# Softmax over 32768 columns: the last two stores moved behind the last load on SyncE's queue, and a 512 B packet per DMA engine written at once

## Chip, cores, metric

One core of one Trainium2 chip. The time is the device time of one execution in microseconds. Executions of the same kernel differ, so medians are given with their number of runs and their spread. Each batch of experiments ran on one chip together with the kernel before; the batches ran on different chips.

## The reference

```python
def reference(logits, temperature):            # logits (16, 256, 32768) float32, temperature 1.0
    scaled = logits / temperature
    scaled = scaled - scaled.max(axis=-1, keepdims=True)
    exp_scaled = np.exp(scaled)
    return (exp_scaled / exp_scaled.sum(axis=-1, keepdims=True)).astype(np.float32)
```

## The kernel before

Each row of 32768 is halved, which gives 8192 rows of 16384 values: 64 tiles of 128 partitions, 64 KB (one row) per partition, 8.4 MB per tile. Three buffers hold three tiles. SyncE issues the loads, ScalarE the stores. A tile is treated in pieces: VectorE takes the maximum of a piece, ScalarE its exponential and sum; the pieces and the two halves of a row are combined by small VectorE instructions; then VectorE and ScalarE share the scaling, in place.

(Shortened: lines joined, comments added.)

```python
_LOAD = 16384
_PIECES = (4096, 4096, 4096, 2048, 2048)
_ON_DVE = (4096, 4096, 2048, 0, 0)
_END = 4096
_FINE_STORES = 3
    def load(t):
        n = _END if t in (0, G - 1) else _LOAD          # first and last tile in four pieces
        for s in range(0, W, n):
            nc.sync.dma_start(out=buf[t % _BUFS][:, s : s + n], in_=x[t * P : (t + 1) * P, s : s + n])

    def store(t, a, b):
        n = _END if t >= G - _FINE_STORES else b - a    # last three tiles in pieces of 16 KB per row
        for s in range(a, b, n):
            nc.scalar.dma_start(out=o[t * P : (t + 1) * P, s : s + n], in_=buf[t % _BUFS][:, s : s + n])
    # ... (combine, normalise: max, exp, combine, scale; normalise(1) issues store(0) after its first exp,
    #      normalise(t) ends with store(t), the last tile stores each piece as soon as it is scaled)
    with tc.manual_schedule():
        for t in range(_BUFS):
            load(t)
        for t in range(G):
            normalise(t)
            if t and t + _BUFS - 1 < G:
                load(t + _BUFS - 1)
```

## Time and profile before

| | before |
|---|---|
| time, median of 3 | 2496.59 us (2495.63 to 2496.76) |
| span of the profiled execution | 2493.4 us |
| busy: VectorE, ScalarE | 63%, 55% |
| DMA | 431 GB/s, full in every slice but the last |

The prediction shows and reads the lines. How to read them: q1 and q10 are the DMA queues of SyncE and ScalarE. In the table of windows the last two columns are the share of the 16 DMA engines that was busy and the rate in GB/s. A packet is one transfer in the records, mostly 64 KB (a whole row) or 16 KB (a piece of one). It counts with its whole duration in the window in which it begins, so single short windows may exceed 1.

### The profile page before, as it was taken

To read this page: it belongs to the slowest core of one execution; us is meant where nothing else is said; L and a number is where in the kernel's file an instruction comes from. 1 tells how busy PE (TensorE), PEld (TensorE's weight loads), DVE (VectorE), ACT (ScalarE), POOL (GpSimd) and SP (SyncE) were. 2 spreads that over 40 slices of the span, in tenths; PEclk is the share of its full clock that TensorE was granted. 3 is DMA by queue.
4 is the path that set the end of the run, shared out by engine and by line. 5 is a ranking of instruction groups with operands and counts; after the bars stand their busy time and mean duration, and the time that the engine had idled before them with its cause. 6 is when DMAs were issued, how large, how long until landed. Compare 5 with 4: busy or idle time off the path is not lost.

```text
span 2493.4 us, 2622 instructions
## 1 busy us (share of the span) xinstructions
DVE 1575.8 (63%) x1216; ACT 1367.7 (55%) x895; POOL 0.2 (0%) x4
## 2 busy tenths in 40 slices
DVE  6575665766657666575665755657656566575665
ACT  6464645646556465464554645546455464554654
POOL 0000000000000000000000000000000000000000
DMA  9999999999999999999999999999999999999998
GB/s 421 433 424 436 435 437 424 436 434 437 424 436 435 437 424 436 433 428 435 434 430 433 434 436 427 433 436 431 429 435 437 423 435 437 427 431 437 425 429 379
DMA packets 20612, 1073.91 MB, mean 431 GB/s; under 512 B 2288, under 2 KB 2288, under 8 KB 2288
## 3 DMA queue, kind: packets, MB, share of 16 engines
q10 hardware_dynamic: 10512, 536.88, 49.9%
q1 hardware_dynamic: 10080, 536.88, 49.9%
q14 instruction: 20, 0.16, 0.0%
HBM read 536.87 MB, written 536.87 MB: 431 GB/s over the span
## 4 chain that ended last, share of the span: by engine, by line
DMA 75%; DVE 15%; ACT 9%; issue 0%; SPq 0%; DVEq 0%; ACTq 0%
DMA x<-in_logits_dram 38%; DMA out_dram<-x 37%; DVE nm L103 11%; ACT x L110 7%; DVE x L142 3%; ACT x L146 2%; DVE f L138 0%; SPq L63 0%; ACT ee L123 0%; DVE rS L137 0%; DVE Sh L82 0%; DVE ttj L126 0%; DVE Sh L79 0%; DVEq L191 0%; ACTq L71 0%
## 5 line engine op out<-in xcount | busy, mean ns | idle before, releaser
L103 DVE TENSOR_REDUCE nm<-x 128x1 f32<-128x4096 f32 x318 | 1117.5, 3579 | 678.0 <-DMA x<-in_logits_dram 678.0
L110 ACT ACTIVATE x<-x,nm 128x4096 f32<-128x4096 f32 x318 | 965.3, 3036 | 1026.2 <-DVE nm L103 1013.6
L146 ACT ACTIVATE x<-x,f 128x2048 f32<-128x2048 f32 (+1 forms) x194 | 371.2, 1975 | 75.4 <-DVE f L138 74.1
L142 DVE TENSOR_SCALAR x<-x,f 128x4096 f32<-128x4096 f32 (+2 forms) x194 | 372.2, 1975 | 2.5 <-DVE f L138 0.2
L126 DVE CUSTOM_DVE_ANT_0 ttj<-ee,ssum 128x5 f32<-128x5 f32 (+1 forms) x64 | 10.6, 166 | 203.0 <-ACT ee L123 203.0
L110 ACT ACTIVATION_READ_ACCUMULATOR x<-x,nm 128x1 f32 x318 | 59.2, 186 | 0.0
L123 ACT ACTIVATE ee<-nm,nMh 128x5 f32<-128x5 f32 (+1 forms) x64 | 18.1, 283 | 0.0
L138 DVE TENSOR_SCALAR f<-ee,rS 128x5 f32<-128x5 f32 (+1 forms) x64 | 14.8, 231 | 2.2
L137 DVE RECIPROCAL rS<-Sh 128x1 f32<-128x1 f32 x64 | 10.5, 164 | 2.2
L82 DVE TENSOR_TENSOR nMh<-nMh 128x1 f32<-128x1 f32 x64 | 10.2, 160 | 2.2
L82 DVE TENSOR_TENSOR Sh<-Sh 128x1 f32<-128x1 f32 x64 | 10.2, 159 | 2.2
L121 DVE TENSOR_REDUCE nMh<-nm 128x1 f32<-128x5 f32 (+1 forms) x64 | 10.1, 157 | 2.2
L79 DVE STREAM_SHUFFLE nMh<-nMh 128x1 f32<-128x1 f32 x64 | 9.7, 151 | 0.0
L79 DVE STREAM_SHUFFLE Sh<-Sh 128x1 f32<-128x1 f32 x64 | 9.7, 151 | 0.0
L110 ACT ACT_TABLE_LOAD x1 | 1.3, 1283 | 8.1 <-DMA x<-in_logits_dram 8.1
L126 DVE DVE_READ_ACCUMULATOR2_ANT Sh<- 128x1 f32 x64 | 5.3, 83 | 0.0
L79 DVE LOAD_MASK_SELECT Sh<-Sh x64 | 0.9, 14 | 2.8
L79 DVE LOAD_MASK_SELECT nMh<-nMh x64 | 0.9, 14 | 2.8
L177 POOL MEMSET const-bfloat16-1.0<- 128x1 bf16 x1 | 0.1, 101 | 0.0
L177 POOL MEMSET const-uint8-127<- 128x1 uint8 x1 | 0.1, 101 | 0.0
L177 POOL MEMSET const-float32-0.0<- 128x1 f32 x1 | 0.1, 98 | 0.2 <-issue 0.2
L177 POOL MEMSET const-float32-1.0<- 128x1 f32 x1 | 0.1, 98 | 0.0
## 6 DMA issues: line engine op xcount, KB each, us to landing
out_dram<-x ACTq DMA_DIRECT2D x12, 2048.0 KB, 19.3
x<-in_logits_dram SPq DMA_DIRECT2D x8, 2048.0 KB, 18.4
x<-in_logits_dram SPq DMA_DIRECT2D x62, 43.6
out_dram<-x ACTq DMA_DIRECT2D x61, 44.3
```

The source lines that it names most:

```text
L79: nc.vector.stream_shuffle(out=v[:, j + 1 : j + 2], in_=v[:, j : j + 1], mask=mask)
L82: nc.vector.tensor_tensor(out=v[:, j + 1 : j + 2], in0=v[:, j : j + 1], in1=v[:, j + 1 : j + 2], op=op,)
L103: nc.vector.tensor_reduce(out=nm[:, k : k + 1], in_=xc, axis=X, op=A.max, negate=True)
L110: nc.scalar.activation(out=xc, in_=xc, func=Exp, bias=nm[:, k : k + 1], scale=inv_t, accum_out=ssum[:, k : k + 1],)
L121: nc.vector.tensor_reduce(out=nMh[:, 0:1], in_=nm, axis=X, op=A.min)
L123: nc.scalar.activation(out=ee, in_=nm, func=Exp, bias=nMh[:, n_rounds : n_rounds + 1], scale=-1.0)
L126: nc.vector.tensor_tensor_reduce(out=ttj, in0=ee, in1=ssum, scale=1.0, scalar=0.0, op0=A.mult, op1=A.add, accum_out=Sh[:, 0:1],)
L137: nc.vector.reciprocal(out=rS, in_=Sh[:, n_rounds : n_rounds + 1])
L138: nc.vector.tensor_scalar_mul(out=f, in0=ee, scalar1=rS)
L142: nc.vector.tensor_scalar_mul(out=xs[:, a:b], in0=xs[:, a:b], scalar1=f[:, k : k + 1])
L146: nc.scalar.activation(out=xs[:, b:c], in_=xs[:, b:c], func=Copy, scale=f[:, k : k + 1])
L177: nc = _bacc.Bacc("TRN2", target_bir_lowering=False, num_devices=1)
```

## The change

Its intent is to keep the DMA engines busy at the end (the last load no longer shares them with the store of tile 62, and ScalarE no longer stands in its waits), and to pay for the first use of the store queue early.

```diff
-_FINE_STORES = 3
+_TOUCH = 128
+    touch = pool.tile([16, _TOUCH], fp32, tag="touch", name="touch")
     def store(t: int, a: int, b: int) -> None:
-        n = _END if t >= G - _FINE_STORES else b - a
-        for s in range(a, b, n):
-            nc.scalar.dma_start(
-                out=o[t * P : (t + 1) * P, s : s + n],
-                in_=buf[t % _BUFS][:, s : s + n],
-            )
+        engine = nc.sync if t >= G - 2 else nc.scalar
+        engine.dma_start(
+            out=o[t * P : (t + 1) * P, a:b], in_=buf[t % _BUFS][:, a:b]
+        )
     with tc.manual_schedule():
+        nc.vector.memset(touch, 0.0)
         for t in range(_BUFS):
             load(t)
+        nc.scalar.dma_start(out=o[:16, :_TOUCH], in_=touch)
         for t in range(G):
```

Store 61 stays on ScalarE's queue but goes out as whole rows of 64 KB; store 62 is one DMA on SyncE's queue; store 63 keeps its four pieces, on SyncE's queue.

## The prediction

> **What bounds the kernel now.** I read the page's slices and queue shares first, then the chain of waits, then the time line of the last 60 us, then short windows at both ends, and last the packet records of the trace.
>
> ```profile
> DMA  9999999999999999999999999999999999999998
> DMA packets 20612, 1073.91 MB, mean 431 GB/s; under 512 B 2288, under 2 KB 2288, under 8 KB 2288
> q10 hardware_dynamic: 10512, 536.88, 49.9%
> q1 hardware_dynamic: 10080, 536.88, 49.9%
> ```
>
> The 16 DMA engines are full in every slice but the last; q1 holds the loads (issued by SyncE), q10 the stores (issued by ScalarE), and each takes half of the engines' time. So this is a DMA-bound stream, and only idle or stretched DMA time can be won. In the packet records a 64 KB packet (one partition's whole row) takes 2.418 us and a 16 KB packet 0.611 us. Each engine has to move 67.1 MB: 16 engines at 65,536 B in 2.418 us make 433.7 GB/s, and 1073.7 MB at that rate take 2476 us. The span is 2493.4 us, the measured time 2496.59 us, so some 3.2 us lie outside the span and at most 17 us inside it could be anything but plain transfer. 2% would be 50 us: not to be had.
>
> Where the 17 us are: about 9.5 us per engine are 64 KB packets that ran longer than 2.418 us (scattered, except one cluster, below); 1.75 us pass before the first packet; some 1.3 us follow the last; the rest is a hole near the end. The hole in windows (columns: busy time by engine, clock, DMA share, GB/s):
>
> ```profile
> 2462.00:2464.00 2.00, 0.00 (x0) 2.00 (x1) 0.00 (x0) 1.00 1.03 442
> 2464.00:2466.00 2.00, 0.00 (x0) 2.00 (x3) 0.00 (x0) 1.00 0.82 352
> 2466.00:2467.00 1.00, 0.00 (x0) 1.00 (x1) 0.00 (x0) 1.00 0.31 131
> 2467.00:2468.00 1.00, 0.00 (x0) 1.00 (x1) 0.00 (x0) 1.00 0.15 66
> 2469.00:2470.00 1.00, 0.69 (x5) 0.23 (x1) 0.00 (x0) 1.00 0.08 33
> 2471.00:2472.00 1.00, 1.00 (x2) 0.44 (x2) 0.00 (x0) 1.00 0.00 0
> 2472.00:2473.00 1.00, 1.00 (x2) 1.00 (x1) 0.00 (x0) 1.00 0.84 360
> ```
>
> Most engines run dry at 2465.5 to 2467 and start again at 2472.4, with the store of the last tile (63). A share of about 0.06 is one engine of sixteen: one engine goes on alone until 2470.4 (its packets end at that time in the records). Why the last store is late:
>
> ```profile
> 2439.82 13.70 ACTq L71 DMA_DIRECT2D out_dram<-x  x3
> 2440.89 17.39 DVE L103 TENSOR_REDUCE nm<-x 128x1 f32<-128x4096 f32 x4
> 2453.56 3.71 ACT L110 ACTIVATE x<-x,nm 128x4096 f32<-128x4096 f32 x1 [12.54 <-DMA x<-in_logits_dram]
> ...
> 2468.34 0.28 ACT L123 ACTIVATE ee<-nm,nMh 128x4 f32<-128x4 f32 x1
> ...
> 2471.52 0.34 ACTq L71 DMA_DIRECT2D out_dram<-x  x1
> ```
>
> ScalarE is stuck from 2439.8 to 2453.5 in issuing tile 62's store. The program order says why: its four pieces reuse the completion semaphores of the four pieces of load 63, so each piece waits until one of those has landed. All four exponentials of tile 63 then run in a row after 2453.56 (14.9 us), though VectorE had its maxima ready one by one from 2445.3.
>
> **What the Trainium skill says.** "DMA: Bandwidth & Descriptors", section "Queues, rings and completion order": each DMA engine takes turns between the queues that have work, one packet at a time. The trace agrees. In 2404 to 2408 us, with 64 KB load packets against mostly 16 KB store packets, q1 has 68.4% and q10 17.2% of the engines (packets counted by start); from 2414 to 2450, both with 16 KB, 51.2% and 49.8%. The same page, "Issuing engines are not separate DMA queues": DMAs issued from different engines run on the same 16 engines. Agrees: q10 alone from 2456 to 2464 moves 436 GB/s, no less than both together, so moving stores to SyncE's queue costs no bandwidth. Same page, "Where 436 GB/s comes from": a ceiling of 435 GB/s; the 433.7 above is that ceiling for practical purposes. I found nothing there on the first use of a queue, which the added packet is about.
>
> **The change part by part.**
> (1) Store 62 goes from ScalarE's queue to SyncE's, behind load 63, as one DMA. ScalarE no longer stands in its semaphore waits. The compiled order shows no such wait left on ScalarE; the pieces of store 63 wait for semaphores of load 62, store 60 and the first two pieces of load 63, all landed by then. Load 63 no longer shares the engines with store 62, only with store 61. Store 61 has 64 KB packets now and load 63 16 KB ones, so the load gets about a fifth until store 61 is through, then everything: both are done at the same sum. From before: everything up to store 62 was done at 2466 (2470.4 on the slow engine), and store 62 is 8 rows of 2.418 = 19.35 us per engine, so load 63 lands near 2446.5 (2451 on the slow engine) instead of 2453.1. Tile 62 is computed at 2441.0, so store 62 is in the queue in time and no hole opens there.
> (2) The end of tile 63 then hangs on VectorE: its four maxima start at 2440.89, after tile 62's scaling, and end at 2458.32 as before (the last piece would have to land after 2453.9 to delay them). Then exp 3.78, and from the ee exponential to the first store issue 3.18 as before (2468.34 to 2471.52): 2458.35 + 3.78 + 3.18 = 2465.3 instead of 2471.5, that is 6.2 us earlier; first packets at about 2466.2 (0.85 us after the issue, as before).
> (3) The fast engines now hardly idle: dry at about 2465.5, fed at 2466.2. They gain about 6.2 us. But the slow engine idled only from 2470.4 to 2472.4. It gains 2.0 us, and the end is the slowest engine's: the last packet goes from 2492.05 to 2490.05. The 0.1 to 0.2 us spread of landings at the end of before is an effect of the hole, which let the slow engine catch up.
> (4) Stores 61 and 62 as 64 KB packets: 16 rows per engine, each 4 x 0.611 - 2.418 = 0.026 us cheaper, 0.42 us; six semaphore packets of 9 ns fewer, 0.05 us. An instruction-fetch packet (8 KB, 0.31 to 0.47 us) that fell into the hole may now cost an engine 0.3 us. Net +0.2 us won.
> (5) The added packet. In before the first store is issued at 46.52, and the 16 load packets that begin at 48.4 to 48.8 take 2.9 to 3.6 us instead of 2.418, on average 0.94 us more on all 16 engines. The windows show it as the one share over 1 at the same GB/s:
>
> ```profile
> 40.00:45.00 5.00, 2.94 (x1) 0.00 (x0) 0.00 (x0) 1.00 0.97 419
> 45.00:50.00 5.00, 5.00 (x2) 3.48 (x1) 0.00 (x0) 1.00 1.16 419
> 50.00:55.00 5.00, 5.00 (x2) 4.12 (x4) 0.00 (x0) 1.00 0.97 419
> ```
>
> That looks like a price of the store queue's first use. The first load packets at 1.75 us likewise take about 1.25 instead of 0.611 us. The added store (16 rows of 512 B, one per engine, after a VectorE memset of about 0.1 us) should be issued near 0.9 us and reach the engines near 2.2 us, where they are still slow with the loads' own start. If the two first-use prices overlap, up to 0.94 us is won; if not, the price is only moved, and nothing is won. I take 0.6. The packet itself is under 0.1 us per engine; the wait of store 0 on its landing is over 40 us early.
>
> Sum: 2.0 + 0.2 + 0.6 = 2.8 us; 2496.6 - 2.8 = 2493.8 us.
>
> **Rivals.** (a) The lag of the slow engine is chance and not a property of the run: then the end moves with the first store's issue, 6.2 + 0.2 + 0.6 = 7.0 us, 2489.6 us. For it: only one trace. Against it: the eighteen 8 KB instruction-fetch packets of 0.309 us between 100 and 2342 us make 5.6 us, near the 4.5 us of lag, if one engine carries them all; which engine carried a packet is not recorded. And store landings show one engine 6.5 to 8 us after the first nearly everywhere. (b) Load 63, at a fifth of the engines, lands later than 2453.9 and delays VectorE's last maximum, so ScalarE's freedom is worth less: 2495 to 2497 us. Against it: the sum of bytes ahead of it is smaller than before. (c) The first-use price is tied to the first large write, not to the queue: the touch wins nothing, 2494.4 us. (d) SyncE's queue with loads and stores in a row stalls at the change of direction: 1 to 2 us, about 2495.5 us. (e) The steady stream changes its rhythm by the shift of semaphores and timing: it is at the ceiling, so only the scattered 9.5 us can move, by perhaps 1 us either way.
>
> **Range and chances.** The centre is 2493.8; (a) pulls down, (b) and (d) up, and runs of before spread by 1.1 us. 8 in 10: 2489.3 to 2496.4. Within 2% is practically certain: 0.5% each side is for a fault that I don't see.
>
> **What the profile of after would show.** Step 1: no ScalarE wait near 2440 to 2453, load 63 landed by about 2452. Step 2: the first store of tile 63 issued near 2465 (less what the touch wins). Step 3: no window with DMA share under 0.9 between 2440 and 2485, but the last 5 us of transfers running on one or a few engines, the landings of the last stores spread by 4 to 5 us instead of 0.2. Step 5: the window 45 to 50 us back at 0.97 and the DMA share or GB/s of the first 5 us a little worse. Wrong: if the last landings lie close together and the end is 6 to 7 us earlier, rival (a); if the stretched packets at 48 us remain, rival (c).

## The result

The changed kernel took 2496.78 us (median of 4 runs: 2502.03, 2498.99, 2494.58, 2493.97), the kernel before in the same comparison 2496.21 (4 runs, 2495.63 to 2496.76). The ratio is 1.0005, 95% interval 0.9986 to 1.0024: the same. "Within 2%" was right, but 2496.78 lies outside the predicted range of 2489.3 to 2496.4, by 0.4 us.

The profiled execution is the slowest of the four. From its page: traffic, queues, and the landings of the stores and of the added packet (last column: us from issue to landing).

```profile
span 2500.3 us, 2620 instructions
DMA packets 19781, 1073.93 MB, mean 430 GB/s; under 512 B 2208, under 2 KB 2224, under 8 KB 2224
q1 hardware_dynamic: 10800, 553.65, 51.4%
q10 hardware_dynamic: 8960, 520.11, 48.5%
...
out_dram<-touch ACTq DMA_DIRECT2D x1, 8.0 KB, 5.8
out_dram<-x SPq DMA_DIRECT2D x1, 28.6
```

16.8 MB of stores moved from q10 to q1, and the added packet landed 5.8 us after its issue. (Its packets reached the engines at 5.4 to 5.9 us, not near 2.2 us as forecast, so they missed the slow start of the loads that they were to overlap with.) The engines were as full as before, yet the span is 6.9 us longer. The issue of the last load in the kernel before, and the end of the execution of the changed one, from their time lines (start, duration, engine):

```profile
2410.02 2.31 SPq L63 DMA_DIRECT2D x<-in_logits_dram  x4
```

```profile
2418.12 2.53 SPq L65 DMA_DIRECT2D x<-in_logits_dram  x4
2450.99 28.75 SPq L73 DMA_DIRECT2D out_dram<-x  x5
...
2455.29 3.71 ACT L111 ACTIVATE x<-x,nm 128x4096 f32<-128x4096 f32 x1 [4.33 <-DVE nm L104]
...
2468.27 3.71 ACT L111 ACTIVATE x<-x,nm 128x4096 f32<-128x4096 f32 x1 [0.52 <-DVE nm L104]
2471.97 0.28 ACT L124 ACTIVATE ee<-nm,nMh 128x4 f32<-128x4 f32 x1
```

and from its windows:

```profile
45.00:50.00 5.00, 5.00 (x2) 3.43 (x1) 0.00 (x0) 1.00 1.18 419
...
2472.00:2474.00 2.00, 1.53 (x8) 0.85 (x3) 0.00 (x0) 1.00 0.00 0
2474.00:2475.00 1.00, 1.00 (x2) 1.00 (x2) 0.00 (x0) 1.00 0.15 66
2475.00:2476.00 1.00, 1.00 (x1) 1.00 (x1) 0.00 (x0) 1.00 0.58 246
...
2496.00:2497.00 1.00, 0.00 (x0) 0.00 (x0) 0.00 (x0) 1.00 0.08 33
2497.00:2498.00 1.00, 0.00 (x0) 0.00 (x0) 0.00 (x0) 1.00 0.08 33
```

Three readings. First, the end does what was forecast, only later. SyncE issues load 63 as soon as store 60 has landed: at 2418.12 here, at 2410.02 in the kernel before, so 8.1 us of delay had gathered before the changed part began. ScalarE's exponentials now follow VectorE's maxima one by one, and the first piece of store 63 was issued at 2475.01, which is 56.9 us after load 63's issue; in before it was 2471.52 - 2410.02 = 61.5 us. (A share of 0.00 in 2472 to 2474 doesn't mean idle engines: their packets had begun before. The packet records have fifteen of them dry at about 2473.6 and fed again at 2475.9: 2.2 us, where 0.7 was forecast.) Second, the last stretch of transfers is that of one engine alone (one of sixteen is a share of 0.06; the windows show 0.08, as a packet counts where it begins), as forecast. Third, the window at 45 to 50 us still shows a share of 1.18 at 419 GB/s: the stretched packets at the first store are all there.

So what is to be explained is the 8 us lost in the stream of tiles, which the change hardly touches, and the scatter of 8 us between four runs.

### The profile page after: what moved, and what is told of

The parts are those of the page before. It is cut to its first block, busy times and chain, and to the rows that moved or that the text cites. A ratio compares the mean times of both kernels' runs of the same rounds, so it can differ in the third digit from the quotient of the medians.

```text
span 2500.3 us, 2620 instructions
## 1 busy us (share of the span) xinstructions
DVE 1575.7 (63%) x1217; ACT 1367.8 (55%) x895; POOL 0.2 (0%) x4
## 4 chain that ended last, share of the span: by engine, by line
DMA 73%; DVE 16%; ACT 9%; another core or an unknown queue 2%; issue 0%; SPq 0%; ACTq 0%
DMA x<-in_logits_dram 37%; DMA out_dram<-x 36%; DVE nm L104 12%; ACT x L111 7%; DVE x L143 3%; ACT x L147 2%; DVE f L139 0%; ACT ee L124 0%; DVE rS L138 0%; DVE Sh L83 0%; DVE ttj L127 0%; DVE Sh L80 0%; SPq L65 0%; ACTq L196 0%
## 5 line engine op out<-in xcount | busy, mean ns | idle before, releaser
L127 DVE CUSTOM_DVE_ANT_0 ttj<-ee,ssum 128x5 f32<-128x5 f32 (+1 forms) x64 | 10.6, 166 | 196.8 <-ACT ee L124 196.8
```

The source lines that it names most:

```text
L127: nc.vector.tensor_tensor_reduce(out=ttj, in0=ee, in1=ssum, scale=1.0, scalar=0.0, op0=A.mult, op1=A.add, accum_out=Sh[:, 0:1],)
```

## Experiments

Two measures come from the trace's packet and semaphore records. *Stretched time*: the durations of the 64 KB packets beyond 2.418 us, summed and divided by 16 engines. *Tail*: from the landing of store 60 on the slowest of the 16 engines to the last landing of all. Up to store 60 both kernels do the same work but for the added packet, so the tail isolates the moved stores. A DMA has sixteen landings, one semaphore update from each engine. The records don't name the engine: "the slowest engine" is the last of the sixteen updates, and that it is the same engine from one DMA to the next is supposed.

### Is the scatter the kernel's own? (the change repeated, and each part alone)

The changed kernel again, no edit:

> The changed kernel as it is, five rounds beside the kernel before, to see whether its spread (2493.97 to 2502.03 us in four runs, against 2495.63 to 2496.76) is its own. Theory A (the steady stream of this kernel varies because of the added packet, which sets another rhythm of the two queues from the start): spread over 5 us again, median 2495 to 2499. Theory B (the spread was chance of that chip or that hour): spread under 2 us and a median of 2493 to 2495, as predicted. In the profile the load packets near 48 us should again be stretched by about 1 us under both.

The added packet alone:

```diff
 (kernel before; cut: _TOUCH and the tile touch, as in the change)
+        nc.vector.memset(touch, 0.0)
         for t in range(_BUFS):
             load(t)
+        nc.scalar.dma_start(out=o[:16, :_TOUCH], in_=touch)
```

> The kernel before plus the added packet alone (memset and one 16 x 512 B store at once; the stores of the end untouched). Theory A: the wide spread comes along, 2496 to 2504 us, median 2498 or more, with 12 us or more of stretched 64 KB packets per engine in the profile (9.5 in before). Theory B: like before, 2495.5 to 2497 us.

The moved stores alone:

```diff
 (changed kernel)
-        nc.vector.memset(touch, 0.0)
-        nc.scalar.dma_start(out=o[:16, :_TOUCH], in_=touch)
```

> The changed kernel without the added packet: only the stores of the last tiles changed. Up to 2400 us it is the kernel before. Theory A: narrow spread and 2493 to 2494.5 us, 2 to 3 us under before. Theory B: the same time as the changed kernel, 2493 to 2495 us. A third theory (C: the moved stores win nothing, as the slow engine decides): 2495.5 to 2497 us.

Measured in one batch, all correct: before 2496.92 (11 runs, 2493.32 to 2503.99); changed 2493.96 (5 runs, 2492.19 to 2497.0), ratio 0.9986 [0.9971, 1.0001]; packet alone 2493.41 (5 runs, 2492.52 to 2497.4), 0.9987 [0.9970, 1.0004]; moved stores alone 2493.58 (6 runs, 2491.92 to 2503.56), 0.9995 [0.9976, 1.0015]. Here the kernel before itself spread over 10.7 us. The scatter belongs to none of the versions, and theory A (the packet brings it) falls; theory B's narrow spread of under 2 us was a miss too (4.8 us for the changed kernel), and so was its 2495.5 to 2497 for the packet alone. No interval excludes 1. Times alone could not tell the parts apart: the packet alone has as low a median as the moved stores. The traces could:

| trace | span | stretched per engine | store 60 landed (slowest engine) | last landing | tail |
|---|---|---|---|---|---|
| before | 2493.4 | 9.5 | 2409.9 | 2492.5 | 82.6 |
| before, second trace | 2494.3 | 10.6 | 2411.1 | 2493.5 | 82.4 |
| packet alone | 2494.2 | 10.3 | 2410.6 | 2493.4 | 82.8 |
| changed | 2500.3 | 17.2 | 2418.0 | 2499.0 | 81.0 |
| changed, again | 2490.4 | 7.6 | 2407.9 | 2489.1 | 81.2 |
| changed, third | 2490.5 | 8.0 | 2408.2 | 2489.2 | 81.0 |
| moved stores alone | 2490.2 | 7.6 | 2407.6 | 2489.0 | 81.4 |

The tail is 82.4 to 82.8 with the old stores and 81.0 to 81.4 with the moved ones, whatever the run's time: the moved stores win 1.5 us (82.6 less 81.1, the means), and the packet nothing. In the other traces with the moved stores, further below, the tail is 80.1 to 81.7. Nearly all the rest of the differences lies before store 60. The price at the first store is there with the packet alone too:

```profile
45.00:50.00 5.00, 5.00 (x2) 3.54 (x1) 0.00 (x0) 1.00 1.16 419
```

The end of the repeated run, windows first, then its time line:

```profile
2462.00:2464.00 2.00, 1.66 (x8) 0.85 (x2) 0.00 (x0) 1.00 0.30 131
2464.00:2465.00 1.00, 1.00 (x2) 1.00 (x2) 0.00 (x0) 1.00 0.15 66
2465.00:2466.00 1.00, 1.00 (x1) 1.00 (x1) 0.00 (x0) 1.00 0.50 213
...
2486.00:2487.00 1.00, 0.00 (x0) 0.00 (x0) 0.00 (x0) 1.00 0.08 33
```

```profile
2408.01 2.60 SPq L65 DMA_DIRECT2D x<-in_logits_dram  x4
```

In this run the first piece of store 63 was issued at 2464.88, again 56.9 us after load 63's issue (2408.01); fifteen engines had landed their last by 2486.1 and the sixteenth at 2489.1.

A second trace of the kernel before (no edit), in a later batch, to test the measure:

> A second trace of the kernel before, for the reading that the span less the mean stretched time per engine is a constant of each kernel: 2483.9 us for before (2483.87 in the first trace, 2483.97 in that with the added packet alone) against 2482.6 to 2483.1 for the changed one. Expected 2483.5 to 2484.3 whatever the time is; if it falls outside, this way of taking the scatter out is not good to half a microsecond.

The span less the stretched time was 2483.8, inside the expectation; the time was 2496.25.

The changed kernel a third time (no edit):

> The changed kernel once more for the size of the scatter: nine runs so far have a median of 2494.57 and the kernel before 2496.2 to 2496.9 in its batches. Expected: median 2493 to 2496, ratio to before 0.998 to 1.000; span less stretched time 2482.5 to 2483.1 us in its trace.

Measured 2492.25 (5 runs, 2490.25 to 2497.24) against 2495.72 (9 runs), ratio 0.9989 [0.9976, 1.0001], just under the expected median. Span less stretched time 2482.5. Over the three comparisons the changed kernel has 14 runs with a median of 2493.97 and the kernel before 24 with 2496.0, 2.0 us apart. With a scatter of 5 to 10 us that is no proof of a gain.

### Packet size or queue?

```diff
 (kernel before)
-_FINE_STORES = 3
+_FINE_STORES = 1
```

Stores 61 and 62 as whole rows, still on ScalarE's queue.

> The kernel before with stores 61 and 62 as whole rows but still on ScalarE's queue: tells the packet size from the queue. Store 62 then waits for one semaphore of load 63 or of none, and competes with load 63. Theory that the queue order matters: load 63 with 16 KB packets is starved by two stores with 64 KB packets, lands near 2465 us and the time is 2500 to 2510 us. Theory that freeing ScalarE is what matters: 2493 to 2495 us.

Measured 2507.53 (6 runs, 2505.18 to 2530.7), ratio 1.0056 [1.0027, 1.0085]: the first theory. The time line of its end:

```profile
2446.10 0.34 ACTq L71 DMA_DIRECT2D out_dram<-x  x1
...
2459.04 3.71 ACT L110 ACTIVATE x<-x,nm 128x4096 f32<-128x4096 f32 x1 [0.53 <-DVE nm L103]
2479.77 3.71 ACT L110 ACTIVATE x<-x,nm 128x4096 f32<-128x4096 f32 x1 [16.93 <-DVE nm L103]
```

ScalarE is free here (store 62 is issued at 2446.1 without a wait), but VectorE, done with three pieces at 2459.0, waits 16.3 us for the last piece of load 63, which comes in 16 KB packets against the 64 KB packets of stores 61 and 62. The tail is 94.6 us. So whole rows on ScalarE's queue are a loss, and neither the packet size nor ScalarE's freedom pays by itself; with store 62 behind the load in the same queue the tail is 1.5 us shorter than before's. The place in the queue with the old 16 KB pieces was not run.

### What is the price at the first store?

A larger early store, 128 rows of 4 KB:

```diff
 (changed kernel)
-_TOUCH = 128
+_TOUCH = 1024
-    touch = pool.tile([16, _TOUCH], ...)
+    touch = pool.tile([P, _TOUCH], ...)
-        nc.scalar.dma_start(out=o[:16, :_TOUCH], in_=touch)
+        nc.scalar.dma_start(out=o[:P, :_TOUCH], in_=touch)
```

> The changed kernel with a bigger added store: 128 rows of 4 KB instead of 16 of 512 B. If the stretch of the 16 load packets at 48 us is a price of the store queue's first rows of some size, on every engine eight of them, it should be gone (the window 45 to 50 us at a DMA share of 0.97). If it is tied to the first full store beginning beside the loads, it stays (1.16 to 1.19, 0.9 to 1.1 us per engine).

The first store came at 48.0 us here (1.4 us later, behind the added traffic) and the stretched packets moved with it, to 50 us: 2.8 to 3.3 us each, 0.64 us per engine on average. That is less than the 0.94 of the first trace, but the second trace of the kernel before, without any early store, has 0.62: that the 0.5 MB written early made the price smaller isn't shown. It didn't go away. The one run took 2493.95. The first full store on the other queue instead:

```diff
 (moved stores alone)
-        engine = nc.sync if t >= G - 2 else nc.scalar
+        engine = nc.sync if t == 0 or t >= G - 2 else nc.scalar
```

> The changed kernel without the added packet and with the first store on SyncE's queue, behind the loads of tiles 1 and 2, so that ScalarE's queue is first used by store 1 near 70 us. If the price is that of a queue's first use beside another busy queue, the stretched packets move to about 72 us. If it is that of the first large write to HBM, whatever the queue, they come when store 0 begins, near 58 us (or in the packets around it), and nothing comes at 72 us.

Its one run took 2493.16. Its windows:

```profile
45.00:50.00 5.00, 5.00 (x2) 3.51 (x1) 0.00 (x0) 1.00 0.97 419
...
55.00:60.00 5.00, 4.89 (x7) 4.85 (x3) 0.00 (x0) 1.00 1.21 419
...
70.00:75.00 5.00, 5.00 (x3) 0.68 (x2) 0.00 (x0) 1.00 0.97 419
```

The stretched load packets (3.2 to 3.9 us) begin at 58 us, the last ones before store 0, and nothing happens when ScalarE's queue is first used by store 1. So in this one trace the price goes with the first full store and not with a queue. A 512 B packet per engine doesn't pay it in advance. Why the first full store has a price is open.

### Loads alone, stores alone

Their outputs are wrong, which doesn't matter for the times. Loads alone: all but the last tile are only loaded and their maxima taken.

```diff
 (moved stores alone, in normalise)
+            if t < G - 1:
+                continue          # after the maximum of each piece
+        if t < G - 1:
+            return                # no combining, scaling, storing
```

> Wrong on purpose: all 64 tiles are loaded and only their maxima taken; only the last tile is stored. If packets are stretched where loads and stores run side by side, the 64 KB load packets show next to no stretched time (under 0.3 us per engine, against 2.9 to 5.3 us for the loads of the whole kernels). If loads are stretched by something else (refresh, fetches, traffic of others), some 2 to 4 us stay.

Stores alone: three tiles are treated, then their buffers are stored over and over.

```diff
 (moved stores alone)
-        for t in range(G):
-            normalise(t)
-            if t and t + _BUFS - 1 < G:
-                load(t + _BUFS - 1)
+        for t in range(_BUFS):
+            normalise(t)
+        for t in range(_BUFS, G):
+            store(t, 0, W)            # all on ScalarE's queue
```

> Wrong on purpose: three tiles are loaded and treated, then their buffers are stored 64 times in a row with no load beside. Side by side theory: under 0.5 us of stretched time per engine in the stores after the first three (against 4.7 to 11.9 us). Otherwise 4 us or more stay. The stretched load packets at the first store should still be there, near 48 us.

They took 1290.6 and 1307.99 us, one run each. By the letter both expectations missed: the stretched time was 2.0 us per engine in the loads and 2.9 in the stores after the first 60 us (1.2 more at the first store, as expected). But it is of another kind: the median packet takes 2.422 instead of 2.418 us, which makes 2 us over 500 packets. Counted are packets over 2.518 us (0.1 us beyond): 13 of 7680 loads, 2 of 8192 stores, together 0.26 us per engine. The seven traces of the table have 255 to 513 of them after the first 60 us, 6 to 16 us per engine (978 and 39 us in one run below). So hardly any long packets come without loads and stores in one stream. Whether it takes their standing side by side, or the loop in which each waits for the other through the compute engines, these two runs, one trace each, don't separate.

### What paces the slowest engine?

The slowest engine lands a store every 38.6 us, but at every seventh tile about 1.0 us late, right after an 8 KB instruction-fetch packet (queue q14 in the page). Between these steps it loses nothing: 38.6 us are its 8 rows of a load and 8 of a store, 16 packets at 2.414 us (most begin 4 ns before the last has ended). In the repeated run eight steps, at the landings of stores 8, 14, 21, 28, 34, 41, 48 and 55, each follow a fetch packet; the eleven other fetch packets before store 60 have no step. In the first trace of the moved stores one of the eight fetches came a tile later, and its step, at store 35, too. If fetches pace it, a longer program must cost time. On GpSimd, which is idle:

```diff
 (changed kernel, after normalise(t); cut: the tile idle)
+            nc.gpsimd.tensor_copy(out=idle[:, 1:2], in_=stat[t % _SETS]["rS"])
+            for _ in range(39):
+                nc.gpsimd.memset(idle[:, 0:1], 0.0)
```

> The changed kernel with 40 tiny instructions more per tile on the idle GpSimd (2560 in all), which do nothing but lengthen the program. In the traces one engine lands its last store 3.0 us after the other fifteen, and 64 KB packets are stretched most in the 100 us after an 8 KB instruction-fetch packet (20 of them in all). Theory F (the fetches make the slow engine, as the prediction supposed): some 20 fetch packets more, and the last landing 9 us instead of 3 us after the fifteenth, time up by about 6 us. Theory G (the fetches also set off the stretching): stretched time per engine 14 us or more instead of 7.6 to 9. Theory H (the fetches have nothing to do with either): as the changed kernel, last landing 3 us late, 2492 to 2497 us.

Measured 2492.65 (5 runs, 2491.93 to 2494.67; before beside it 2496.07, 9 runs; ratio 0.9985 [0.9971, 0.9998], the only interval of all that lies under 1): theory H by the time. But two engines, not one, landed 1.9 us after the others. So three times the dose (`range(119)`):

> Three times the dose of the run with 40 idle GpSimd instructions per tile (7680 in all, some 60 fetch packets more of 0.31 us). There two engines, not one, landed last, 1.9 us after the others. If GpSimd's fetches all ride on one DMA engine, and that one adds them to its transfers, it now has 18 us more to do and the time goes up by 12 to 16 us. If they are spread over the engines, or taken up by the others' waiting, the last landings stay within 4 us of the first and the time within 2 us of the changed kernel (2492 to 2497).

Measured 2518.08 (4 runs, 2517.45 to 2518.4; ratio to before 1.0089 [1.0074, 1.0105]), 26 us more than the changed kernel on the same chip (2492.25), and more than the 12 to 16 expected. GpSimd's work itself didn't slow VectorE: a maximum of 4096 columns takes 4.41 us on VectorE in this trace and in the repeated run. Its page and windows:

```profile
q14 instruction: 81, 0.66, 0.1%
```

```profile
1055.00:1060.00 5.00, 0.00 (x0) 0.00 (x0) 3.15 (x33) 1.00 0.85 328
1060.00:1065.00 5.00, 0.00 (x0) 0.00 (x0) 3.15 (x33) 1.00 1.09 472
```

81 fetch packets instead of 21. In the stretch from 1055 to 1060 us fifteen engines have finished their load; the first packet of the next store, begun at 1057, takes 2.5 to 3.3 us on each of them. The sixteenth is still busy with its load row and lands the previous store at 1060.85; only then can SyncE issue the next load (1060.97). The packets of the fifteen follow each other without a gap, so the time that they give up to keep the sixteenth's pace can only lie in such longer packets; that these contain a wait is an inference, and how it comes about isn't in the records. Then the dose on the other two programs, 18 idle instructions per tile each:

```diff
 (moved stores alone, after normalise(t); in both runs cut: the tile idle and its memset)
+            for _ in range(18):
+                nc.scalar.activation(out=idle[:, 0:1], in_=idle[:, 1:2], func=Copy)
```

> The moved stores, with 18 idle ScalarE instructions per tile more (program 641 to 1793 instructions, some 9 fetches more); ScalarE has the 3.6 us per tile free. If ScalarE's fetches ride on the slowest DMA engine, 1 us each: 8 to 10 us more, 2501 to 2504 us, with the 1 us steps at every second or third tile. If they ride on another engine with time to spare: up to 2 us more.

```diff
 (moved stores alone, after normalise(t))
+            for _ in range(18):
+                nc.vector.memset(idle[:, 0:1], 0.0)
```

> The same dose on VectorE (18 tiny memsets per tile, program 1090 to 2243 instructions, some 9 fetches more, about 1.1 us of VectorE's time per tile, which lengthens a tile's treatment by nothing before its store). If VectorE's fetches ride on the slowest DMA engine: 8 to 10 us more, 2501 to 2504 us. If not: up to 2 us more. Only one of the two programs need be the one; if both cost 8 us or more, both ride on it.

On one chip: ScalarE's program longer, 2496.52 (4 runs, 2493.78 to 2499.15); VectorE's longer, 2501.86 (4 runs, 2500.86 to 2503.14); before 2498.19 (11 runs, 2493.57 to 2508.17). The ratios to before are 0.9995 [0.9973, 1.0017] and 1.0013 [0.9994, 1.0031]: neither is clear of the noise. How the slowest engine landed stores 36 to 56 (us beyond 38.59 from one store to the next, from the semaphore records):

```
changed, again        0.0 0.0 0.0 0.0 0.0 1.0 0.0 0.0 0.0 0.0 0.0 0.0 1.0 0.0 0.0 0.0 0.1 0.1 0.0 1.0 0.0
ScalarE dosed         0.0 0.0 0.0 0.2 0.5 0.4 0.0 0.4 0.0 0.0 0.2 0.6 0.4 0.0 0.4 0.0 0.0 0.2 0.5 0.1 0.1
VectorE dosed         0.0 0.0 1.1 0.0 0.0 0.3 0.7 0.0 0.0 1.0 0.0 0.4 0.5 0.7 0.0 0.0 1.0 0.0 0.0 1.0 0.0
GpSimd, 120 per tile  0.7 0.7 0.7 0.7 0.7 0.7 0.7 0.2 0.5 0.6 0.6 0.6 0.6 0.7 0.7 0.8 0.7 0.9 0.7 0.7 0.7
changed (slow run)    0.0 0.1 0.3 1.0 1.1 1.0 0.0 0.4 0.2 0.2 0.0 0.5 1.7 0.0 0.4 0.1 0.0 0.9 0.9 1.3 0.0
```

VectorE's dose doubles the steps, and that is the evidence; the time is weaker. From store 2 to 60 its slowest engine took 2260.2 us, 10 us more than in the two quick traces of the changed kernel (2250.0 and 2250.5) and in that of the moved stores (2249.8), but the changed kernel's slow first trace took 2259.8 without any dose. ScalarE's dose took 2251.5 and left two engines late at the end (last landings at 2490.6 and 2490.8, the others by 2488.5). In this batch the two dosed kernels' medians are 5.3 us apart, and their four runs each don't overlap. That fits a picture in which each engine's program is fetched through a DMA engine of its own and VectorE's engine is the last by a little. The mapping itself is inferred: the records don't name the DMA engine. Each fetch costs its engine more than its own 0.31 us, as the data packet that begins right after it is stretched too (2.6 to 3.0 us instead of 2.418 in the repeated run).

### Does a shorter program give time back?

Four pieces (ScalarE 517 instructions instead of 641, VectorE 1028 instead of 1090), then three (VectorE 904), both with the moved stores alone:

```diff
-_PIECES = (4096, 4096, 4096, 2048, 2048)
-_ON_DVE = (4096, 4096, 2048, 0, 0)
+_PIECES = (4096, 4096, 4096, 4096)      # second run: (8192, 4096, 4096)
+_ON_DVE = (4096, 4096, 2048, 0)         # second run: (8192, 2048, 0)
```

> The moved stores without the added packet, and the tiles between the first and the last in four pieces of 4096 columns instead of five, which shortens ScalarE's program from 641 to 517 instructions and VectorE's from 1090 to 1028. In the traces the slowest DMA engine lands a store every 38.6 us, and about 1.0 us later at every seventh tile, just after an instruction fetch; so a shorter program should need fewer such delays. Theory F2 (the fetches of one engine's program pace the slowest DMA engine, 1 us each): 1 to 2 us under the moved stores alone, so 2490.5 to 2493 us, and the 1 us steps at every eighth to ninth tile if ScalarE's program is the one, still at about every seventh if it is VectorE's. Otherwise the same time as the moved stores alone, 2492 to 2495 us.

> A version that might beat both: the moved stores without the added packet, and three pieces (8192, 4096, 4096) in the middle tiles, so that VectorE's program, whose fetches pace the slowest DMA engine, has 904 instructions instead of 1090. If about 1 us per fetch is right and VectorE's the program that counts, the 1 us steps come at every eighth to ninth tile instead of every seventh, and the time is 1 to 2 us under the moved stores of the same batch. If the later end of each tile (ScalarE's exponentials end some 3 us later) makes the slowest engine wait, it is 2 us or more slower.

Beside the three pieces, the moved stores once more (no edit):

> The moved stores without the added packet once more, beside the kernel before and the three pieces on the same chip: median 2 to 3 us under the kernel before of the same rounds (the first time 2493.58 against 2496.92, the changed kernel 2493.96), if the chip's scatter leaves it visible; span less stretched time 2482.4 to 2482.9 us in its trace.

Four pieces: 2495.38 (6 runs), ratio 0.9987 [0.9971, 1.0004], no better than the changed kernel's 0.9986. Three pieces: 2501.38 (6 runs, 2496.73 to 2509.19) on a chip where the moved stores took 2501.17 (6 runs, 2494.09 to 2526.78) and the kernel before 2498.04 (11 runs, 2494.66 to 2517.41). The steps did move to every eighth tile, as the shorter program asks, but nothing can be said of the time: the expected 1 to 2 us drown. The expected 2 to 3 us that the moved stores were to win was a miss here (ratio to before 1.0017 [0.9976, 1.0058]). I have no version that beats both kernels beyond doubt.

That chip gave the clearest sight of the scatter. The profiled run of the moved stores took 2526.78 us (stretched time 41 us per engine, tail 80.1, span less stretched time 2484.0 instead of the expected 2482.4 to 2482.9, so that measure fails in so disturbed a run). Its two halves, beside those of the first run of the same kernel:

```profile
300.00:1300.00 1000.00, 617.80 (x480) 537.83 (x355) 0.00 (x0) 1.00 1.00 420
1300.00:2300.00 1000.00, 628.83 (x487) 543.31 (x357) 0.00 (x0) 1.00 1.00 431
```

```profile
300.00:1300.00 1000.00, 634.26 (x488) 546.81 (x357) 0.00 (x0) 1.00 1.00 434
1300.00:2300.00 1000.00, 631.13 (x493) 547.95 (x362) 0.00 (x0) 1.00 1.00 433
```

The same program ran at 420 GB/s for its first half and at 431 afterwards; the first run held 434 and 433. The slowest engine lost 0.6 to 2.3 us (once 4.5) at nearly every tile from store 6 on, and from about 1300 us on much less. The first run of the same program shows no such episode, so the program alone doesn't fix when it comes. What makes it is open: nothing in these traces names it, and work of other cores on the chip, which they don't record, isn't excluded.

## Why the prediction was wrong, point by point

- **The steps of the moved stores held in the main.** Part (1): no ScalarE wait is left, and load 63 landed at 2460.3 in the first trace, 42.2 us after its issue; counted from before's issue that is 2452.2, against "2451 on the slow engine" and the check "by about 2452". Part (2) held in kind: the first store was forecast at 2465.3 and came at 2464.9 and 2464.7 in two runs. But that is luck: their streams were 2.0 and 2.3 us ahead of before's when load 63 was issued. Counted from that issue the forecast is 55.3 us, and all four traces show 56.9 to 57.0, a gain of 4.6 us and not 6.2. The forecast took the start of tile 63's maxima "as before"; it comes 1.8 us later, as the last landing of load 62 does (4.8 us after load 63's issue in the four traces, 3.0 in the three with the old stores). It goes with the whole rows of store 61, whose packets take 2.418 us now and took 0.611: the run with whole rows on ScalarE's queue, where nothing else was changed, has the 4.8 us too (load 63 issued at 2413.24, the maxima of tile 62 from 2418.05). Part (3): the slowest engine sets the end; it landed 2.7 to 3.1 us after the fifteenth in these four traces (4 to 5 forecast), which refutes rival (a). Rival (b) didn't happen, and rival (d) is not seen: on the slowest engine store 62 landed 19.3 us after load 63 (2479.6 after 2460.3), the time of its 8 packets.
- **The sum of parts (3) and (4) was mis-sized a little:** 2.2 us forecast, 1.5 measured as the difference of tails. The missing part lies before load 63's landing, which came 41.8 to 42.4 us after its issue on the slowest engine where part (1) had 41.0; from there to the end the first trace has 38.7 us, store 62 and store 63 at 19.3 us each, so nothing was left to win there.
- **Part (5) failed: "I take 0.6".** The packet won nothing; rival (c) was right as far as the runs go. The packet-alone trace has the share of 1.16 at 45 to 50 us that before has, and before's tail.
- **The step that put the result outside the range is rival (e) with the sentence on the spread:** "it is at the ceiling, so only the scattered 9.5 us can move, by perhaps 1 us either way", and "runs of before spread by 1.1 us". Measured in its place: stretched time of 7.6 to 17.2 us between traces of the changed kernel (41 in one of its moved stores alone), and runs of before from 2492.8 to 2504.0 in the three comparisons. Three close runs were taken for the spread of the kernel. What makes the scatter stays open. In hindsight, with a term of some 4 us either way the same centre would have held 2496.78.
- **The centre was near, partly by luck:** 2.8 us were forecast under before, and the tails give 1.5. The 2.0 us between the medians of 14 and 24 runs don't confirm it: in its batch the packet alone, which wins nothing in its tail, lies 3.5 us under before.
- **Slips without effect:** "some 3.2 us lie outside the span" set the median of three runs against the span of another run. In that run itself it is 1.9 (2495.3 less 2493.4). And the fetch packets between 100 and 2342 us are nineteen, not eighteen.
- **"The DMA engines are full" was too simple.** They were busy in every window, but at less than the full rate: the fast engines' packets are longer where they have to keep the slowest one's pace, and the slowest is set back about 1 us by certain instruction fetches. The prediction saw the slow engine and suspected the fetches. It supposed that one engine carries them all; the dosed runs point to one DMA engine per program, which is inferred.

## What to carry to other kernels

When a stream looks full, look at what the slowest of the parallel engines does: it alone sets the end, and filling the others' holes wins only what it wins (here 1.5 us, though the last store begins 4.6 us earlier). To judge an effect of a few microseconds in milliseconds, find an interval in the trace that contains only the change (the tail here); the medians of five runs could not separate 1.5 us from none. And put an instruction count on the list of costs where transfers are the limit: 7680 idle instructions on GpSimd cost 26 us here, while 2560 cost nothing measurable.

## What the Trainium skill lacked or had wrong

- "Runtime: NRT & Kernel Launch", section "Instruction fetch mechanics", has the fetches of a long program and calls their cost mostly hidden; what they cost data transfers on a full DMA stream it doesn't say. Here 60 more fetch packets of GpSimd's cost 26 us, and the data packet right after a fetch took 2.6 to 3.0 us instead of 2.418.
- "Perfetto Trace Analysis", section "DMA Engine Tracks", says that slices show actual busy time without idle. In these traces busy time isn't always transfer at the full rate: the DMA share is 1.00 in both halves of one run that moved 420 and 431 GB/s, and fifteen engines take up to 3.3 us for a store packet instead of 2.418 while the sixteenth catches up. That waiting is counted in it is inferred.
- No page has the price of the first full store: 0.6 to 1.2 us per engine (1.35 in the most disturbed run), in the load packets in flight, on either queue, and not removed by a small store ahead.
- No page speaks of the scatter of a transfer-bound kernel with one core in use: the same program took 2494.1 to 2526.8 us in six runs on one chip.
